# A hybrid decoder layer on one core: when the transfers that sum weight blocks are issued

## The chip, the core and the metric

The kernel runs on one core of a Trainium2 chip. The metric is the device time of one execution in microseconds (us). The core has a matrix engine (PE), a vector engine (DVE), a scalar engine (ACT), a general engine (POOL) and a synchronisation engine (SP) that here only issues DMAs. Each engine takes its instructions in the order of its own queue. Sixteen DMA engines move the bytes; SP and POOL issue to different DMA queues.

## What is computed

One trunk layer over 512 positions of width 1024, in f32:

```python
h = rms_norm(x, norm_mix)
hq, hf, hi, hg, mq, mk, mv = split(h @ w_in)        # 7 x 512 columns
o_hgrn = hgrn2_mixer(hq, hf, hi, hg, lb, hgrn_norm) # gated linear recurrence, 4 heads
o_moba = moba_attention(rotary(mq), rotary(mk), mv) # block-sparse causal attention, 4 heads
x = x + concat(o_hgrn, o_moba) @ w_out
h, mem_n = rms_norm(x, norm_xattn), rms_norm(mem, norm_mem)
x = x + cross_attention(h, mem_n, w_xq, w_xk, w_xv, w_xo)   # 256 memory tokens, 4 heads
h = rms_norm(x, norm_mlp)
x = x + square(relu(h @ w_ff1)) @ w_ff2             # 1024 -> 4096 -> 1024
return rms_norm(x, norm_final)
```

## The kernel before

**Weights come in units.** A unit is 512 KB of a weight matrix, 128 partitions by 1024 f32. It is loaded into a tile `wr` (three buffers), then split for PE into an upper part `wh`, made by ACT with a copy to fp32r, and a lower part `wl = wr - wh`, made by DVE. A product is three matmuls: upper by upper, upper by lower, lower by upper. Units 0 to 27 are the columns of `w_in`, by stage: hf (0 to 3), hi (4 to 7), hq (8 to 11), mv (12 to 15), mkq (16 to 23), hg (24 to 27). Units 28 to 79 follow the list `line`: the eight units of `w_out` (wo), the eight of `w_xq` (xq) and the eight of `w_xo` (xo), with 28 units of the memory's keys and values (`memX`, `memY`) put between those of wo and xq by `AFTER_WO` and `AFTER_XQ`: wo is units 28 to 32, 36, 39 and 43; xq is 46, 49, 52, 55, 58, 62, 65 and 67; xo is 72 to 79. Then follow the two matrices of the MLP.

**How units are fed.** Before the matmuls of unit `w`, `need(w)` issues loads and splits ahead of it. With three raw buffers a unit is split two units ahead and loaded some five ahead; a load waits on SP until `wl` of the unit three before it has been made. `need` also notes in `marks` the last matmul issued so far.

**Sums of weight blocks.** The memory's keys and values and the second MLP matrix are multiplied by a scheme with seven products in place of eight, whose weight operands are sums of blocks. These sums are made in DRAM by DMAs alone. `mem_sums` and `block_sums` list 88 transfers. A copy goes out on SP (line 237). An add, which accumulates into its destination, goes out on POOL (line 240). The pieces of value blocks, two DMAs of 256 KB to a transfer, go out on POOL as well (line 269). In the order of the list:

- 0 to 3 pieces and 4 to 7 adds that make the first memory sum;
- 8 to 11 copies that begin the third memory sum, 12 to 15 pieces that begin the fourth;
- 16 to 19 copies of the first sum into the second, 20 to 27 adds to the second and third, 28 to 31 adds of the second sum to the fourth;
- 32 to 47 copies and 48 to 63 adds for the MLP's sums, 64 to 87 the rest of them.

**Which sets the order.** `load_unit` issues the load of unit `u` and then `sums_after(u)` transfers of the list, by `more_sums`. Each of them is made to wait for `marks[-2]`; for the transfers behind unit `u` that is the end of the matmuls of unit `u - 7`. A copy that waits on SP holds up what stands behind it there, later loads among it. The list's order also carries data: an add waits for the landing of what it adds to, and the loads of the summed units (`wr<-m`, `wr<-u`) for the sums. The very first part, and the MLP, run in an order written out by hand (`manual_schedule`); between them the framework's scheduler orders each engine's queue. `Pace` is the kernel's own estimate of time, by which side work such as attention heads is put among the matmuls; `copy` and `add` go to the engines directly, past its records.

**Side work that the steps touch.** In hq, `ev_q` scales the query of an HGRN2 head into the tiles `qx` and `q` on DVE, and `hgrn_out` multiplies these on PE (tiles `ket`, `a`, `pd`, `ho`). In xq, `xattn_probs` makes scores on PE (`xs`), their minimum on DVE (`xum`), the exponentials on ACT (`xp`), and turns these on PE (`xt`). Nearly every compute instruction is recorded under line 118, the helper that calls the engine, so groups are told apart by their tiles.

Of the kernel before, what the change touches and what calls it, by code (L numbers as in the profile page):

```python
# [31 lines left out]
W_HG, W_WO, W_MEMK, W_XQ, W_MEMV, W_XO, W_MLP = 24, 28, 36, 44, 52, 60, 68  # L32
# [93 lines left out]
def hybrid_layer(ctx: ExitStack, tc: tile.TileContext, xT, memT, ws, vecs, consts, rots, out):  # L126
# [91 lines left out]
    line, keys = [], iter(KEYS + VALUES)  # L218
# [96 lines left out]
    def load_unit():  # L315
        u = state["load"]
        raws[u] = raw_tile(f"wr{u}", u >= FF2 and (u - FF2) % 2 == 1)
        if len(sources[u].shape) == 3:
            SY.dma_start(raws[u].rearrange("p (n c) -> p n c", n=4), sources[u])
        else:  # L320
            SY.dma_start(raws[u], sources[u])
        state["load"] += 1
        for _ in range(sums_after(u)):
            more_sums()

    def sums_after(u):

        if u < W_WO:
            return 2 * (u >= 8) + (u >= 22)
        if u < MLP:  # L330
            return line[u - W_WO][0] in ("wo", "xo")
        return u % 2 == 0 and (4 <= u - FF2 < 14 or u - FF2 >= 26)

    W_MV = 12
# [432 lines left out]
    u = 4  # L767
# [614 lines left out]
    u = MLP  # L1382
# [437 lines left out]
```

## Time and profile before

| | |
|---|---|
| median of 3 runs | 727.66 us (727.19 to 728.85) |
| the profiled execution, its own time | 727.53 us |
| its span, first to last instruction | 725.8 us |
| mean granted clock of PE | 0.992 |
| largest wait of PE | 4.7 us |
| waits of ACT for loads of `wr` | 22.3 us in 16 |

The span is what the trace covers; the time of an execution is some 1.7 us longer. In the views, a row of the timeline gives start and duration in us, then engine, line, operation, what it writes and reads, and in brackets how long the engine was idle before it and what ended that. A row of the waits gives the sum, the count and the longest. A row of the chain of waits gives start, duration, engine and what it worked on. A row of DMA issues gives their count, size, and the median time from issue to landing. `SPq` is SP's own queue. A load's row tells when it was issued, not when it landed.

### The profile page before, as it was taken

How to read it: one execution, taken by the hardware profiler on the slowest of the kernel's cores; microseconds unless marked ns; L12 is line 12 of the kernel's file. 1: busy time of each engine (PE TensorE's matmuls, PEld its weight loads, DVE VectorE, ACT ScalarE, POOL GpSimd, SP SyncE). 2: the span in 40 equal slices, each digit the busy share in tenths (PEclk: the TensorE clock that was granted, in tenths of full speed). 3: DMA queues.
4: the chain of work that ended last, by engine and by line, in shares of the span. 5: the costliest groups of instructions: out<-in, count | busy, mean ns of one | idle time of the engine just before them, and what ended most of it. 6: DMA issues, size and time to landing. Idle time of an engine off the chain costs nothing.

```text
span 725.8 us, 10723 instructions
## 1 busy us (share of the span) xinstructions
PE 712.3 (98%) x4024; PEld 613.6 (85%) x4024; DVE 579.2 (80%) x878; ACT 452.5 (62%) x659; POOL 81.1 (11%) x98
## 2 busy tenths in 40 slices
PE   9997999999999999999999999999999999999995
PEld 7885888888888888888888899999999888888885
DVE  5897635899879676786668799989899999987886
ACT  6873467455777576666656866666567755546672
POOL 1421123000000000001201011111120100110000
PEclk9999999999999999999999999999999999999998
DMA  8798689994557864557997388777989965998523
GB/s 273 239 254 297 197 159 203 348 338 119 145 184 206 243 229 154 174 168 182 262 279 178 99 224 216 210 216 201 220 191 284 290 233 183 278 266 258 179 84 116
DMA packets 62803, 155.71 MB, mean 215 GB/s; under 512 B 5248, under 2 KB 19456, under 8 KB 62240
## 3 DMA queue, kind: packets, MB, share of 16 engines
q1 hardware_dynamic: 47552, 116.70, 46.2%
q0 software_dynamic: 14592, 37.75, 28.8%
q8 instruction: 31, 0.51, 0.3%
q10 hardware_dynamic: 608, 0.59, 0.3%
q14 instruction: 20, 0.16, 0.1%
HBM read 152.92 MB, written 48.23 MB: 277 GB/s over the span
## 4 chain that ended last, share of the span: by engine, by line
PE 90%; DMA 4%; ACT 3%; DVE 2%; issue 1%; DVEq 0%; SPq 0%; ACTq 0%
PE Y L118 16%; PE X L118 12%; PE xo L118 8%; PE XB L118 6%; PE XA L118 6%; PE mkq L118 6%; PE wo L118 6%; PE xq L118 4%; DMA wr<-in_ws_dram 4%; PE mv L118 3%; PE hg L118 3%; PE Z L118 3%; PE hf L118 3%; PE memX L118 3%; PE memY L118 2%; PE hq L118 1%
## 5 line engine op out<-in xcount | busy, mean ns | idle before, releaser
L118 DVE TENSOR_TENSOR wl<-wr,wh 128x1024 fp32r<-128x1024 f32 (+2 forms) x139 | 165.7, 1197 | 39.8 <-ACT wh L118 33.2
L118 ACT ACTIVATE wh<-wr 128x1024 fp32r<-128x1024 f32 (+2 forms) x139 | 142.8, 1037 | 85.3 <-DMA wr<-in_ws_dram 22.3
L240 POOL DMA_DIRECT2D u<-in_ws_dram x32 | 27.4, 874 | 319.1 <-DMA wr<-m 88.3
L118 PE MATMUL X<-op,wh 128*128 128x512 f32 (+1 forms) x264 | 62.9, 385 | 0.0
L118 PEld LDWEIGHTS X<-op,wh 128*128 128x128 f32 x264 | 47.2, 189 | 8.5
L118 PE MATMUL Y<-op,wh 128*128 128x512 f32 x192 | 47.2, 391 | 0.0
L118 PEld LDWEIGHTS Y<-op,wh 128*128 128x128 f32 x192 | 35.0, 189 | 6.5
L118 PEld LDWEIGHTS X<-op,wl 128*128 128x128 f32 x256 | 33.5, 191 | 1.6
L118 PE MATMUL X<-op,wl 128*128 128x256 f32 x256 | 34.1, 283 | 0.0
L118 PE MATMUL Y<-OS,wh 128*128 128x256 f32 x256 | 33.4, 283 | 0.0
L118 PEld LDWEIGHTS Y<-OS,wh 128*128 128x128 f32 x256 | 32.5, 192 | 0.7
L118 DVE TENSOR_TENSOR op<-g,op 128x1024 fp32r<-128x1024 f32 x24 | 29.3, 1220 | 2.8 <-ACT op L118 2.8
L118 ACT ACTIVATE op<-g 128x1024 fp32r<-128x1024 f32 x28 | 29.3, 1045 | 0.6 <-PE XB L118 0.6
L118 ACT ACT_TABLE_LOAD x20 | 25.7, 1283 | 2.1 <-PEq L1808 1.2
L118 PEld LDWEIGHTS Y<-op,wl 128*128 128x128 f32 x192 | 25.3, 191 | 1.3
L118 PE MATMUL Y<-op,wl 128*128 128x256 f32 x192 | 25.7, 282 | 0.0
L118 PE MATMUL mkq<-xlo,wh 128*128 128x512 f32 x64 | 25.7, 401 | 0.0
L118 PE MATMUL xq<-x1hi,wl 128*128 128x512 f32 x64 | 25.6, 400 | 0.0
L118 PE MATMUL mkq<-xhi,wl 128*128 128x512 f32 x64 | 25.4, 396 | 0.0
L118 PE MATMUL xq<-x1hi,wh 128*128 128x512 f32 x64 | 25.3, 396 | 0.0
L118 PE MATMUL mkq<-xhi,wh 128*128 128x512 f32 x64 | 25.3, 395 | 0.0
L118 PE MATMUL xo<-oxhi,wh 128*128 128x512 f32 x64 | 25.1, 393 | 0.0
(384 smaller groups left out, 1908.6 us busy)
## 6 DMA issues: line engine op xcount, KB each, us to landing
wr<-in_ws_dram SPq DMA_DIRECT2D x87, 512.0 KB, 5.5
u<-in_ws_dram POOLq DMA_DIRECT2D x32, 512.0 KB, 7.7
wr<-u SPq DMA_DIRECT2D x32, 512.0 KB, 4.4
u<-in_ws_dram SPq DMA_DIRECT2D x16, 512.0 KB, 12.1
wr<-m SPq DMA_DIRECT2D x16, 512.0 KB, 3.7
m<-in_ws_dram POOLq DMA_DIRECT2D x12, 512.0 KB, 10.6
m<-in_ws_dram POOLq DMA_DIRECT2D x16, 256.0 KB, 7.4
wA<-in_ws_dram SPq DMA_DIRECT2D x8, 512.0 KB, 5.6
```

The source lines that it names most:

```text
L118: return f(*args, **kw)
L240: return nc.gpsimd.dma_start(dst, src, accum_op=ALU.add, max_dma_last_dim=4 * D)
```

## The change

`sums_after(u)` gives other numbers of transfers. Units 12 to 15 have none behind them, where each had two; the eight loads of xq have one each, where they had none. The list and its order, the adds' and copies' queues and the rule of the marks stay. All transfers from the ninth on (number 8) are so attached to later loads, until the counts agree again at the first unit of xo with number 54.

```diff
     def sums_after(u):
 
         if u < W_WO:
-            return 2 * (u >= 8) + (u >= 22)
+            return 2 * (8 <= u < 12 or u >= 16) + (u >= 22)
         if u < MLP:
-            return line[u - W_WO][0] in ("wo", "xo")
+            return line[u - W_WO][0] in ("wo", "xo", "xq")
         return u % 2 == 0 and (4 <= u - FF2 < 14 or u - FF2 >= 26)
```

`W_WO` is 28, `MLP` is 80. The numbers of the transfers behind the loads:

| behind unit | before | after |
|---|---|---|
| 8 to 11 | 0 to 7 | 0 to 7 |
| 12, 13 | 8 to 11 | none |
| 14, 15 | 12 to 15 | none |
| 16, 17 | 16 to 19 | 8 to 11 |
| 18, 19 | 20 to 23 | 12 to 15 |
| 20, 21 | 24 to 27 | 16 to 19 |
| 22 to 25 (three each) | 28 to 39 | 20 to 31 |
| 26, 27 (three each) | 40 to 45 | 32 to 37 |
| the eight of wo | 46 to 53 | 38 to 45 |
| the eight of xq | none | 46 to 53 |
| the eight of xo | 54 to 61 | 54 to 61 |

## The prediction

> **What bounds the kernel now.** First the page: how much of the span TensorE (PE) leaves empty, and which DMA queues carry the weights.
>
> ```profile
> span 725.8 us, 10723 instructions
> PE 712.3 (98%) x4024; PEld 613.6 (85%) x4024; DVE 579.2 (80%) x878; ACT 452.5 (62%) x659; POOL 81.1 (11%) x98
> q1 hardware_dynamic: 47552, 116.70, 46.2%
> q0 software_dynamic: 14592, 37.75, 28.8%
> ```
>
> PE is empty for 13.5 us, so an edit that only moves DMAs can win in two ways: by removing a wait of PE, or by keeping its clock up. The waits of PE and of its weight loads (PEld) name the places.
>
> ```profile
> PE a L118 <- DVE qx L118: 4.7, 1, 4.7
> PEld xt L118 <- ACT xp L118: 0.9, 2, 0.5
> ```
>
> The first is by far the largest. It lies in the stage of unit 8 to 11 (hq), where the decay products `a` of the first HGRN2 head need `qx` from VectorE (DVE). The timelines of PE, DVE and ScalarE (ACT) around it, then the chain that ended last:
>
> ```profile
> 65.06 0.43 PE L118 MATMUL a<-qx,kt 128*32 128x32 f32 x8
> 70.19 0.37 PE L118 MATMUL a<-qx,Fz 128*32 128x96 f32 x3 [4.71 <-DVE qx L118]
> 63.95 0.42 DVE L118 TENSOR_TENSOR qx<-hq,eb 128x256 f32<-128x256 f32 x1
> 68.57 1.23 DVE L118 TENSOR_TENSOR wl<-wr,wh 128x1024 fp32r<-128x1024 f32 x1 [4.20 <-ACT wh L118]
> 69.92 0.22 DVE L118 TENSOR_TENSOR qx<-qx,ee 128x64 f32<-128x64 f32 x1
> 71.25 0.22 DVE L118 TENSOR_TENSOR qx<-qx,ee 128x64 f32<-128x64 f32 x1
> 74.20 0.42 DVE L118 TENSOR_TENSOR q<-qx,pp 128x256 f32<-128x256 f32 x1
> 61.00 0.64 ACT L118 ACTIVATE lnf<-lnf 128x512 f32<-128x512 f32 x1 [0.57 <-DVE lnf L118]
> 67.48 1.06 ACT L118 ACTIVATE wh<-wr 128x1024 fp32r<-128x1024 f32 x1 [5.85 <-DMA wr<-in_ws_dram]
> 52.22 15.16 DMA wr<-in_ws_dram
> 71.53 0.95 PE a L118 x12
> 78.58 1.04 PE a L118 x28
> ```
>
> Read it backwards. PE waits 4.71 us for `qx`. DVE had begun `qx` at 63.95, but next in its queue stands the lower part `wl` of a weight unit, and DVE waits there 4.20 us for the upper part `wh`. ACT could have made that at 61.64, when `lnf` ends; it waits 5.85 us for a load issued at 52.22 that took 15.16 us. Counting loads of `wr` on SP, it is unit 12. PE itself needs that unit only when hq is done: the load hurts because it heads two queues.
>
> The clock pays as well (columns: stretch, its length, busy time of PE, PEld, DVE, ACT, POOL, granted clock, DMA share, GB/s).
>
> ```profile
> 69.00:70.00 1.00, 0.00 (x0) 0.00 (x0) 1.00 (x3) 1.00 (x2) 0.00 (x0) 0.61 0.03 12
> 75.00:76.00 1.00, 1.00 (x6) 0.90 (x6) 0.27 (x1) 0.83 (x2) 0.00 (x0) 0.50 1.02 330
> 76.00:77.00 1.00, 1.00 (x6) 0.83 (x5) 0.78 (x3) 0.08 (x1) 0.00 (x0) 0.98 0.82 276
> ```
>
> PE went idle at 65.49. The grant fell some 3.7 us later (a mean of 0.61 in 69 to 70 puts the fall to 0.5 at about 69.2) and returned at 76.0, 5.8 us after work resumed. The Trainium skill, "TensorE: Matmul & The Clock Gate", section "What's actually happening", says that an idle window of about 3.4 us halves the clock and a busy one of the same length restores it. The fall agrees; the return took 5.8 us here, so the measurement decides, and by the page's figure the gain below would be about 1.2 us smaller, some 723.6 us in all (an estimate).
>
> What made the load slow are the DMAs issued just around it, of SP (line 237) and POOL (line 269):
>
> ```profile
> 40.11 1.33 SPq L237 DMA_DIRECT2D m<-in_ws_dram  x2
> 49.43 2.07 SPq L237 DMA_DIRECT2D m<-in_ws_dram  x2
> 51.26 3.00 POOL L269 DMA_DIRECT2D m<-in_ws_dram  x4 [12.98 <-PE hi L118]
> 56.02 2.94 POOL L269 DMA_DIRECT2D m<-in_ws_dram  x4 [1.75 <-PE hq L118]
> wr<-in_ws_dram SPq DMA_DIRECT2D x7, 512.0 KB, 3.3
> ```
>
> These are exactly transfers 8 to 15 of the sum list, which `sums_after` now gives to units 12 to 15: four copies of 512 KB and eight pieces of 256 KB. The last row, from the DMA answer for 284 to 316 us where no sums run, is the same kind of load undisturbed: 3.3 us.
>
> **The change part by part.** No instruction is added or removed: 88 transfers stay, each on its queue. Transfers 8 to 53 come later in the order of loads, and from the first xo load on both orders agree.
>
> *Units 12 to 15, emptied.* DVE's chain ahead of unit 12's load is untouched, so that still leaves at 52.2. Undisturbed it lands at 55.5; sums 4 to 7 may still linger, but it could take 9.4 us before ACT, free at 61.64, would notice. `wh` ends at 62.7, `wl` starts when DVE reaches it at 64.37, and DVE runs 4.20 us earlier. PE then resumes 4.20 us earlier, at 65.99. The second half of `a` needs the `qx` that ended at 71.47, now 67.27; its 0.95 us at half clock become 0.48, so `a` ends at 67.8 in place of 72.48: 4.7 us. With PE idle under 2 us the clock should stay: the 3.5 us from 72.48 to 76.0 become 1.76. **Gain 4.7 + 1.75 = 6.4 us.** Against it stands DVE, nearly full from 68.6 on, which follows by 4.2 us and perhaps no more. But `a` of the second head starts on PE at 78.58, and its DVE work was done by 74.62 (the `q` of the DVE rows): 4 us of slack take up the other 2.2. I count the full 6.4; the lower end is 4.2.
>
> *Units 16 to 21 (mv and mkq weights are then on PE).* Units 16 and 17 get four DRAM copies in place of four, 18 and 19 small pieces in place of four adds, 20 and 21 copies in place of adds. Twelve adds move to units 22 to 25. From the queue rows 512 KB on q0 take 0.288 x 725.8 / 37.75 x 0.524 = 2.9 us of the sixteen engines, on q1 1.5 us: this stretch gets lighter, then denser.
>
> ```profile
> 85.00:118.00 33.00, 33.00 (x277) 28.11 (x276) 16.29 (x29) 24.73 (x32) 9.26 (x8) 1.00 0.82 157
> 118.00:160.00 42.00, 42.00 (x202) 35.04 (x201) 34.02 (x84) 21.67 (x41) 4.60 (x4) 1.00 1.05 322
> 203.00:262.00 59.00, 59.00 (x264) 48.77 (x262) 46.10 (x58) 41.53 (x59) 2.44 (x3) 1.00 0.71 210
> 262.00:335.00 73.00, 72.91 (x372) 60.81 (x371) 52.38 (x85) 50.77 (x92) 1.62 (x2) 1.00 0.54 170
> wr<-in_ws_dram SPq DMA_DIRECT2D x3, 512.0 KB, 8.8
> ```
>
> The load row is of 85 to 117, where two adds stand beside each load. From 118 to 160 the DMA engines are full already, with copies ahead of the loads on SP; adds go on the other queue instead, so a load there should be nearer that row. PE is never empty in either stretch (33.00 of 33, 42.00 of 42). Zero, covered by loads issued long before PE needs them; 2 us worse if the cover goes.
>
> *wo (unit 28 to 43).* Two copies and six adds become eight copies, 1.5 us each in place of 2.9. PE has no empty time there (59.00 of 59), so the relief is worth nothing. The copies wait on SP for the marks of PE's progress that the adds waited for on POOL, and the next load stands behind them; but a mark lies seven units back and a load is issued some five units ahead, so the mark has passed when SP gets there. Zero; up to 2 us if SP is held.
>
> *xq (unit 46 to 67): the cost.* Two copies and six adds enter a stage with none. Adds go by a mark, the end of the matmuls seven units earlier. The third is due after unit 51:
>
> ```profile
> 278.56 0.39 PE L118 MATMUL memY<-wh,mo 128*128 128x512 f32 x1
> 276.75 5.80 DMA wr<-in_ws_dram
> 282.63 1.07 ACT wh L118
> 283.73 1.23 DVE wl L118
> 284.95 0.34 DVE xum L118
> 286.68 0.44 PE xt L118 x2
> 267.46 1.06 ACT L118 ACTIVATE wh<-wr 128x1024 fp32r<-128x1024 f32 x1
> wr<-m SPq DMA_DIRECT2D x1, 512.0 KB, 4.2
> ```
>
> This is the hq pattern again: the load of unit 55 holds `wh`, `wl` stands in DVE's queue before `xum`, and PE's transposes `xt` wait. PE's slack is nil: that is the 0.9 us in the waits. The add leaves at about 279.2, when 3.3 of the load's 5.8 us remain. Ends: nothing, if it moves its bytes after 282.5; the add's whole 2.9 us, if the load gets no turn meanwhile. I take just under half, **1.3 us**. Below nothing is excluded, as nothing on this chain gets earlier but ACT's `wh` of 267.46, which had no wait. That one is unit 50 (last row: issued at 262.22, landed 266.42, 1.04 us early); a copy and an add beside it can eat this and more, 0 to 3.4 us; I take 0, since units 39 to 45 load faster now and their chain arrives earlier.
>
> **Sum:** 727.53 (the profiled execution; span 725.8 and 1.7 around it; the median shown is 727.66) - 6.4 + 1.3 = **722.4 us**.
>
> **The rivals.**
> 1. *The adds take equal turns with the loads.* Unit 55 then pays 2.9 us, unit 50 0.5 beyond its slack: 727.5 - 6.4 + 3.4 = 724.5. For it: loads beside adds took 8.8 us against 3.3. Against: only the last part of the load is met. The Trainium skill, "DMA: Bandwidth & Descriptors", section "Queues, rings and completion order", says that each engine goes round the queues that have work, packet by packet; by that rule this rival wins. That loads among adds are slow, not starved, agrees.
> 2. *The wait stays.* The moved copies of units 16 and 17 need only PE's end of units 9 and 10, and the order on SP is the scheduler's here, not the written one: it may put them ahead of loads that still wait for a buffer. Or another load heads DVE's queue instead, unit 13's say. Time 727.5, or up to 1.5 less. Against: unit 12 has some 6 us of room.
> 3. *Slower: the clock falls in xq.* If PE stands over 3.7 us at `xt`, the hq dip is repeated: 5.8 us at half clock, 2.9 lost. At a delay of 5 us the loss is 7.9, the gain is spent: 727.5 - 6.4 + 7.9 = 729.0; this decides from 3.7 us on. All copies and adds at full price on units 47, 50 and 55 make 7.8 us, thus at most 731.8. For it: nil slack. Against: it needs every transfer to fall wrong.
>
> **How the numbers follow.** Forecast 0.60 (its own range 720.2 to 724.6: a free or dearer xq, DVE's 4.2), rival 1 0.20, rival 2 0.08, rival 3 0.09, and 0.03 for a larger gain. The range 720.2 to 726.4 takes the first two. A measurement of this kernel tells about 0.2%, 1.5 us, from no change: faster (below 726.2) 0.82, within 0.09, slower 0.09.
>
> **What would show it.** Right: unit 12's load under 8 us, PE's wait for `qx` under 1 us, the clock 1.00 from 62 to 88 us, and a new wait of PE at `xt` of 1 to 2 us. Wrong: a load over 10 us before `qx`; a clock under 0.9 near 285; PE empty time in mkq (over 105 us), where the twelve adds land.

## The result and the profile after

The changed kernel takes 722.64 us, the median of six runs (720.61 to 724.72), against 728.08 us (727.19 to 729.83) for the kernel before on the same chip. The ratio is 0.9927, with a 95% interval of 0.9903 to 0.995: faster by some 0.7%. Single executions that took 879 us or more, at most two of a kernel, are left out of all medians and ratios below. The execution that was profiled took 724.72 us, the slowest of the six; why it was so matters below.

First the page of the changed kernel, then its waits of PE. The counts of the engines' work are those of before.

```profile
span 722.9 us, 10727 instructions
PE 711.8 (98%) x4024; PEld 613.3 (85%) x4024; DVE 578.6 (80%) x878; ACT 451.3 (62%) x659; POOL 81.1 (11%) x98
```

```profile
PE XB L118 <- DVE g L118: 1.7, 1, 1.7
PE xt L118 <- ACT xp L118: 0.5, 1, 0.5
PE a L118 <- DVE qx L118: 0.2, 1, 0.2
```

The 4.7 us at `qx` have become 0.2, and a wait of 1.7 us stands in the MLP that was not there. The timelines of DVE and ACT in hq show why the first went:

```profile
63.03 0.42 DVE L118 TENSOR_TENSOR qx<-hq,eb 128x256 f32<-128x256 f32 x1
63.37 1.22 DVE L118 TENSOR_TENSOR wl<-wr,wh 128x1024 fp32r<-128x1024 f32 x1
```

```profile
60.08 0.63 ACT L118 ACTIVATE lnf<-lnf 128x512 f32<-128x512 f32 x1 [0.56 <-DVE lnf L118]
60.62 1.99 ACT L118 ACTIVATE wh<-wr 128x1024 fp32r<-128x1024 f32 x2
```

ACT makes the upper parts of units 12 and 13 back to back right behind `lnf`, with no bracket: it waits for nothing. DVE's `wl` has no bracket either. The load of unit 12, from the DMA answer for the stretch in which it alone is issued, and the clock (columns as in the same view of before, whose row for these 26 us is the second fence):

```profile
wr<-in_ws_dram SPq DMA_DIRECT2D x1, 512.0 KB, 3.4
```

```profile
62.00:88.00 26.00, 21.28 (x250) 17.39 (x249) 17.16 (x52) 8.45 (x12) 2.15 (x2) 0.87 0.65 225
```

```profile
62.00:88.00 26.00, 25.69 (x311) 21.54 (x313) 19.61 (x51) 11.28 (x18) 3.00 (x4) 1.00 0.61 203
```

The load takes 3.4 us in place of 15.16. PE is busy 25.69 of 26 us in place of 21.28, at a granted clock of 1.00 in place of a mean of 0.87. The 4.4 us less of empty time, and the half clock, at which PE had worked from 70.19 to 76.05 and lost half of these 5.9 us, add up to 7.3 us: that is the gain.

Where it went from there is read from PE's timelines: the start of a stage is the start of the first matmul into its tile. The table gives these starts before, and how far after and the changed kernel's two repeats (`a1_again`, `a2_again`, below) stand from them, in us. Minus is earlier.

| first matmul of | before | after | a1_again | a2_again |
|---|---|---|---|---|
| `a` (in hq) | 65.06 | -0.14 | -0.02 | +0.97 |
| `mv` | 85.39 | -7.29 | -7.33 | -6.35 |
| `wo` | 203.43 | -7.28 | -7.32 | -6.34 |
| `xq` | 261.09 | -7.32 | -7.36 | -6.38 |
| `xt` (in xq) | 286.68 | -6.47 | -6.81 | -6.63 |
| `xo` | 337.87 | -6.35 | -6.80 | -6.61 |
| `XB` (MLP) | 413.78 | -6.34 | -6.81 | -6.64 |
| `X` (second MLP matrix) | 560.78 | -2.79 | -6.80 | -6.63 |
| end of span | 725.75 | -2.81 | -6.80 | -6.63 |

So the change wins some 7.2 us between `a` and `mv`, keeps them through mkq, hg and wo, gives back up to 1 us in xq (nothing in `a2_again`), and in the one execution that was profiled first 3.5 us more are lost in the MLP, where the order of the transfers is the same as before. Neither repeat shows that last loss.

### The profile page after: what moved, and what is told of

Its sections match the earlier page's. It is cut to its first block, busy times and chain, and to the rows that moved or that the text cites. A ratio compares the mean times of both kernels' runs of the same rounds, so it can differ in the third digit from the quotient of the medians.

```text
span 722.9 us, 10727 instructions
## 1 busy us (share of the span) xinstructions
PE 711.8 (98%) x4024; PEld 613.3 (85%) x4024; DVE 578.6 (80%) x878; ACT 451.3 (62%) x659; POOL 81.1 (11%) x98
## 4 chain that ended last, share of the span: by engine, by line
PE 86%; DVE 5%; DMA 4%; ACT 3%; issue 1%; DVEq 0%; POOL 0%; ACTq 0%; POOLq 0%
PE Y L118 15%; PE X L118 12%; PE xo L118 8%; PE mkq L118 6%; PE XB L118 6%; PE XA L118 5%; PE wo L118 5%; PE xq L118 4%; PE mv L118 3%; PE hf L118 3%; PE hg L118 3%; PE Z L118 3%; PE memX L118 2%; DVE wl L118 2%; PE memY L118 2%; DMA wr<-in_ws_dram 2%
## 5 line engine op out<-in xcount | busy, mean ns | idle before, releaser
L118 PE MATMUL xq<-x1lo,wh 128*128 128x512 f32 x64 | 25.2, 393 | 0.0
```

The source lines that it names most:

```text
L118: return f(*args, **kw)
```

## The experiments

Each kernel was timed beside the kernel before on the same chip. Ratios have 95% intervals.

| kernel | median us | ratio |
|---|---|---|
| the change, again (a1_again) | 721.07 | 0.9892 [0.9864, 0.9919] |
| DVE's order alone (e1_order) | 727.76 | 0.9974 [0.9953, 0.9995] |
| xq for wo (e2_xq_for_wo) | 731.06 | 1.0024 [1.0006, 1.0041] |
| wo twice (e3_wo_twice) | 724.34 | 0.9933 [0.9908, 0.9958] |
| DVE's and ACT's order (e1b_both) | 723.01 | 0.9924 [0.9897, 0.9951] |
| rest at units 14 and 15 only (e4_rest_14_15) | 721.87 | 0.9918 [0.9893, 0.9944] |
| transfers late in xq (e5_xq_late) | 723.58 | 0.9938 [0.9916, 0.9961] |
| the change, one MLP sum later (e6_f1_last) | 722.26 | 0.9917 [0.9893, 0.994] |
| the change, a third time (a2_again) | 721.48 | 0.9916 [0.9887, 0.9945] |
| both orders, one MLP sum later (e8_orders_last) | 720.75 | 0.9905 [0.988, 0.9929] |
| both orders and the change (e9_after_orders) | 721.22 | 0.991 [0.9883, 0.9937] |

### What held PE up in hq: a transfer, or what queued behind it

The prediction says that unit 12's late load hurts only because `wl` stands ahead of `qx` on DVE and `wh` ahead of other work on ACT. If so, the wait goes without moving any transfer when these instructions stand further back. `e1_order` is the kernel before with the lower parts of units 12 and 13 put on DVE behind the last `q` issued until then; in its trace the `q` of the first two heads go ahead of unit 12's. `BEHIND` orders two instructions of one engine without a semaphore.

```diff
         def lower(hi=his[u], lo=los[u]):
-            (eng or V).tensor_sub(lo[:, a:b], raw[:, a:b], hi[:, a:b].bitcast(F32))
+            low = (eng or V).tensor_sub(lo[:, a:b], raw[:, a:b], hi[:, a:b].bitcast(F32))
+            if u in (W_MV, W_MV + 1):
+                tc.add_manual_dep(low.ins, last_q[0].ins.name, BEHIND)
...
-            V.tensor_mul(q4[:, t0 * P:(t0 + 2) * P].rearrange("p (t c s) -> p t c s", c=4, s=CHUNK),
+            last_q[0] = V.tensor_mul(q4[:, t0 * P:(t0 + 2) * P].rearrange("p (t c s) -> p t c s", c=4, s=CHUNK),
```

> The kernel before, no transfer moved; on DVE the lower parts wl of units 12 and 13 go behind the qx and q of the first two heads. Theory (the late load costs only because wl stands in front of qx in DVE's queue): unit 12's load is as late as before (landing near 67), PE's wait for qx falls from 4.7 to under 1 us, the clock stays at 1.00 from 62 to 88 us, time 720.5 to 722.5 (6 to 7 us under before). Rival (the transfers slow hq in more ways than this queue): PE waits elsewhere in hq, gain under 3 us, 725 to 728.

It missed: `mv` starts 1.31 us earlier, not 6 or 7, and the time is 0.9974 of before. The wait at `qx` is gone, but PE's timeline and then ACT's show another in its place.

```profile
70.88 1.65 PE L118 MATMUL pd<-Vh,kets 128*128 128x128 f32 x6 [3.72 <-ACT kets L118]
```

```profile
68.08 1.06 ACT L118 ACTIVATE wh<-wr 128x1024 fp32r<-128x1024 f32 x1 [7.05 <-DMA wr<-in_ws_dram]
69.39 1.06 ACT L118 ACTIVATE wh<-wr 128x1024 fp32r<-128x1024 f32 x1 [0.26 <-DMA wr<-in_ws_dram]
70.35 0.47 ACT L118 ACTIVATE kets<-ket 128x384 f32<-128x384 f32 x1
```

`kets`, the first operand that PE needs from ACT after `a`, stands behind both `wh`. ACT waits 7.05 us for the same load, now 16.4 us long, and PE 3.72 us for ACT; the clock falls to 0.50 again at 70.2. The load headed two queues, and clearing one only showed the other. `e1b_both` therefore also puts both `wh` behind the first head's `kets` on ACT:

```diff
+        if u in (W_MV, W_MV + 1):
+            early_wh.append(rounded)
...
-        A.activation(ket[:, :3 * P], pt[:, :3 * P], AF.Copy)
+        turned = A.activation(ket[:, :3 * P], pt[:, :3 * P], AF.Copy)
+        if h == 0:
+            for made_high in early_wh:
+                tc.add_manual_dep(made_high.ins, turned.ins.name, BEHIND)
```

> The kernel before, no transfer moved. On DVE the lower parts wl of units 12 and 13 go behind the qx and q of the first two heads, and on ACT their upper parts wh go behind kets, the copy that PE's pd waits for. With the DVE order alone PE's 4.7 us at qx became 3.7 us at pd, for kets stood behind wh on ACT. Theory (the late load costs by standing ahead in two queues): unit 12's load is still late (landing 66 to 68), PE waits under 1 us in hq, the clock stays 1.00, mv's first matmul comes 6 to 7.5 us earlier than in the trace of before (at 78 to 79.4 us), time 720.5 to 723. Rival (a third queue or PE itself waits for the late units): mv's first matmul after 82 us, time over 725.

Unit 12's load and the stretch of hq in this kernel:

```profile
wr<-in_ws_dram SPq DMA_DIRECT2D x1, 512.0 KB, 15.0
```

```profile
60.00:90.00 30.00, 30.00 (x365) 25.54 (x364) 23.42 (x66) 14.06 (x22) 2.44 (x3) 1.00 0.91 277
```

The load still takes 15.0 us, and PE has not one empty moment. `mv` starts 7.29 us earlier, and the time is 0.9924. That the change's first trace has the same 7.29 is chance, as `a` starts 0.68 us later in this execution: counted from `a` the orders gain 7.97 us, the change 7.15 to 7.32. The orders gain more since no `wl` stands between the four groups of the first head's `a` any more, which take 1.04 us here and 1.90 in the changed kernel. So the queues are the cause: the transfers only decide how late the instruction at their head can start. Nor do the two remedies add: `e9_after_orders`, with both, gains the same 7.97 us counted from `a`, with `mv` 7.30 us and the end 7.29 us earlier.

> The changed kernel with both orders of e1b as well. If the two remedies act on the same wait, they do not add: mv's first matmul at 77 to 78.2 us, the 0.5 to 1 us of xq stay, time within 1 us of the changed kernel of this call. If units 12 and 13 also cost something behind the queues, 1 to 3 us less.

The 0.5 to 1 us that it expected to lose in xq didn't come: from `xq` to `xo` it loses 0.04.

### Which of the eight transfers made the load late

`e4_rest_14_15` is the kernel before with only the pieces behind units 14 and 15 (POOL's eight DMAs of 256 KB) taken away; the copies behind 12 and 13 stay. Four loads of xq take the four transfers.

```diff
-            return 2 * (u >= 8) + (u >= 22)
+            return 2 * (8 <= u < 14 or u >= 16) + (u >= 22)
...
-            return line[u - W_WO][0] in ("wo", "xo")
+            return line[u - W_WO][0] in ("wo", "xo") or line[u - W_WO] in [("xq", n) for n in range(4, 8)]
```

> Only units 14 and 15 rest (the eight pieces on POOL move on); units 12 and 13 keep their four copies on SP, and only the last four loads of xq take a transfer. If the pieces slow unit 12's load, it lands by 62 and the whole gain in hq stays: mv's first matmul at 78 to 79, time 720.5 to 723. If the copies ahead of it in SP's ring are enough, it lands after 63 and part or all of the wait at qx stays: mv's first matmul at 80 to 85, time 723 to 728.

```profile
wr<-in_ws_dram SPq DMA_DIRECT2D x1, 512.0 KB, 11.4
```

The load of unit 12 takes 11.4 us, PE waits 1.3 us in two places, the clock stays at 1.00, and `mv` starts 5.21 us earlier (5.74 counted from `a`, which was 0.53 later in this execution). With the pieces gone the load is 3.8 us shorter than before; the other 8.0 of its 11.8 us too many stay with the copies. Yet it is not unit 12's load that costs PE the 1.3 us. Two rows of ACT, for units 11 and 12, then the same two units on DVE:

```profile
59.20 1.06 ACT L118 ACTIVATE wh<-wr 128x1024 fp32r<-128x1024 f32 x1 [3.50 <-DMA wr<-in_ws_dram]
63.12 1.06 ACT L118 ACTIVATE wh<-wr 128x1024 fp32r<-128x1024 f32 x1 [0.33 <-DMA wr<-in_ws_dram]
60.30 1.23 DVE L118 TENSOR_TENSOR wl<-wr,wh 128x1024 fp32r<-128x1024 f32 x1 [1.63 <-ACT wh L118]
65.44 1.22 DVE L118 TENSOR_TENSOR wl<-wr,wh 128x1024 fp32r<-128x1024 f32 x1
```

DVE waits for nothing at unit 12. It waits 1.63 us at unit 11, whose load takes 10.8 us here, and all its work for `a` comes later by that. The copies 10 and 11 leave on SP right behind that load. In the six traces of kernels that keep them there it takes 7.9 to 10.9 us, in the seven without them 4.5 to 6.1. So the pieces are worth the larger part of the gain, and what the copies cost beyond them came through the load of unit 11 in this execution.

### What the transfers cost in xq

`e2_xq_for_wo` takes the transfers from wo and gives them to xq, with hq as before, so the cost of xq stands alone.

```diff
-            return line[u - W_WO][0] in ("wo", "xo")
+            return line[u - W_WO][0] in ("xq", "xo")
```

> The kernel before with the eight transfers of wo's loads moved to xq's; units 12 to 15 keep theirs. Theory: hq as before (PE waits 4.7 us), xq pays the 1 us that the changed kernel paid there, 728.5 to 729.5. Within it: if copy 46 ahead of unit 47's load is what costs, that load takes 6 to 7 us in place of 4.3 and DVE waits 2 to 3 us more for it; if the add after unit 51 is what costs, unit 55's load takes over 7 us in place of 5.8. Rival (nothing is paid in xq, the changed kernel's 1 us had another cause): 727 to 728.

The kernel is slower by 0.24%, with an interval that just excludes no change. From `xq` to `xo` it loses 2.0 us (+0.30 to +2.31): PE waits 1.6 us at `xt`, for `xp`. The place is the forecast one, the path is not. The add leaves 1 us after the load of unit 55, on which I had put the cost, but this load takes the 5.8 us of before here, and 4.9 in the changed kernel; the two loads behind it, of units 56 and 57, grow (8.3 and 7.3 us against 5.5 and 4.8). The late ones that count are units 47 and 50, the first with a copy issued ahead of it (6.9 and 5.8 us here). SP's timeline in the changed kernel, then the DMA answers for unit 47's load alone in the changed kernel and before:

```profile
245.81 0.50 SPq L237 DMA_DIRECT2D u<-in_ws_dram  x1
246.56 4.26 SPq L118 DMA_DIRECT2D wr<-in_ws_dram  x3
```

```profile
wr<-in_ws_dram SPq DMA_DIRECT2D x1, 512.0 KB, 7.2
```

```profile
wr<-in_ws_dram SPq DMA_DIRECT2D x1, 512.0 KB, 4.3
```

What that does to DVE, in the timelines of the changed kernel and of before, is the `wl` of that unit:

```profile
254.94 1.23 DVE L118 TENSOR_TENSOR wl<-wr,wh 128x1024 fp32r<-128x1024 f32 x1 [2.99 <-ACT wh L118]
```

```profile
260.96 1.23 DVE L118 TENSOR_TENSOR wl<-wr,wh 128x1024 fp32r<-128x1024 f32 x1 [0.94 <-ACT wh L118]
```

DVE waits 2.05 us more there; unit 50's load follows (5.6 us against 4.2), and what is left of the delay reaches PE at `xt`. The chain of waits that ended last in the changed kernel goes through the loads of units 47, 50 and 55 (some of its rows):

```profile
246.56 7.18 DMA wr<-in_ws_dram
256.19 5.59 DMA wr<-m
271.17 4.92 DMA wr<-in_ws_dram
277.26 1.23 DVE wl L118
280.21 0.44 PE xt L118 x2
```

The other traces with the same transfers agree. Unit 47's load takes 6.2 us in `a1_again`, and 0.55 us are lost from `xq` to `xt`; it takes 5.1 to 5.4 in `a2_again`, `e6_f1_last` and `e9_after_orders`, where nothing is lost on this way. To test the path, `e5_xq_late` is the changed kernel without transfers behind the first two loads of xq, and with two behind each of the last two:

```diff
-            return line[u - W_WO][0] in ("wo", "xo", "xq")
+            name, n = line[u - W_WO][:2]
+            return name in ("wo", "xo") or 2 * (name == "xq" and n > 5) + (name == "xq" and 1 < n < 6)
```

> The changed kernel, but the eight transfers of xq go one each to its third to sixth load and two each to its seventh and eighth; the first two have none. Theory (copies 46 and 47 ahead of the loads of units 47 and 50 cost the 0.5 to 1 us in xq): those loads take 4 to 4.5 us again, the shift of PE's stages against before stays at -7.3 us through xq where the changed kernel's went to -6.3 and -6.8, time 0.5 to 1 us under it. Rival (the add after unit 51, now a copy or a later add, costs it): unit 55's load above 5.8 us, xt still 0.5 to 1 us late.

The first half came as the reading of units 47 and 50 has it: their loads take 3.3 and 3.5 us, and `xt` still starts 7.36 us earlier (`xq` 7.53). But the time is 0.9938, no better. The doubled transfers cost 2.7 us between `xt` and `xo` (-7.36 to -4.62), where the waits of PE show two new ones:

```profile
PE xs L118 <- DVE xql L118: 0.8, 1, 0.8
PE xt L118 <- DVE PT L118: 0.6, 1, 0.6
```

The eight transfers have no free place in xq: put late they cost more than put early.

### Is there room in wo instead?

The prediction costed wo at nothing. `e3_wo_twice` is the changed kernel with the transfers of xq put behind wo's loads, two each.

```diff
-            return line[u - W_WO][0] in ("wo", "xo", "xq")
+            return {"wo": 2, "xo": 1}.get(line[u - W_WO][0], 0)
```

> Units 12 to 15 rest as in the changed kernel, but wo's loads get two transfers each and xq's none. Theory: the gain in hq stays (6.4 to 7.2 us), xq pays nothing, wo has room (PE never empty there): 1 us under the changed kernel where the MLP agrees, 720 to 721.5. Rival (wo has no room: units 39 to 43 have under 2 us between wl and PE): a wait of PE in wo or at xq's start, 722 to 725.

No. `mv` starts 7.08 us earlier, `memX` 7.10, but `xq` only 3.03: 4.1 us are lost before xq begins. PE's waits, then the stretches around them (columns as before):

```profile
PE memY L118 <- ACT wh L118: 1.1, 1, 1.1
PE memY L118 <- DVE wl L118: 0.8, 1, 0.8
```

```profile
244.00:246.00 2.00, 0.93 (x4) 0.37 (x2) 0.32 (x1) 1.18 (x2) 0.00 (x0) 1.00 1.02 377
246.00:248.00 2.00, 1.24 (x6) 0.87 (x6) 2.00 (x3) 1.40 (x2) 0.00 (x0) 1.00 0.15 47
248.00:250.00 2.00, 2.00 (x7) 1.54 (x6) 1.90 (x3) 2.00 (x4) 0.00 (x0) 0.55 0.85 253
```

1.8 us of idle time in two pieces, and then the clock is at 0.55: the waits themselves are under half of the loss. The trace has the clock at half from 248.22 to 251.63, 3.41 us with PE busy throughout, which is 1.7 us more. One transfer to a load is hidden in wo, two are not.

### The loss in the MLP

> The changed kernel once more, for more executions and a second trace. In its first trace 3.5 us were lost in the first MLP matrix, where the load wd took 10.1 us (7.3 before) and PE then waited 1.7 us at a lower clock. Theory (a chance of the execution): the second trace has wd at 7 to 8 us, no wait of PE there and a span of about 719.5 us, and the times lie in two groups some 3.5 us apart, 720.5 to 721.5 and 724 to 725. Rival (the change causes it): wd late again, PE waits 1.5 to 2 us again, span 722 to 723, all times above 722.

The repeat has no such loss: it ends 6.80 us earlier than before, as `xo` starts. The two groups of times didn't come: its five executions took 720.16 to 722.07 us. In the first profile of the change, DVE waits 4.0 us for the tile `wd`, the last block of the first MLP matrix. DVE's timeline there and PE's stretches:

```profile
544.97 1.23 DVE L118 TENSOR_TENSOR wd<-wd,wA 128x1024 f32<-128x1024 f32 x1 [3.95 <-DMA wd<-in_ws_dram]
546.11 1.22 DVE L118 TENSOR_TENSOR wl<-wc,wh 128x1024 fp32r<-128x1024 f32 x1
547.25 0.68 DVE L118 TENSOR_TENSOR g<-g,XB 128x512 f32<-128x512 f32 x1
```

```profile
546.00:548.00 2.00, 0.26 (x4) 0.05 (x2) 2.00 (x4) 1.72 (x2) 0.81 (x1) 1.00 0.03 12
548.00:550.00 2.00, 2.00 (x9) 2.00 (x10) 2.00 (x2) 0.28 (x1) 0.00 (x0) 0.54 0.96 160
550.00:552.00 2.00, 2.00 (x7) 1.53 (x7) 1.93 (x3) 0.07 (x1) 0.00 (x0) 0.60 1.01 281
```

It is the hq pattern a third time: a late load heads DVE's queue, `g` stands behind it, PE is idle for 1.7 us, and the clock halves, from 548.17 to 551.59. The load of `wd` takes 10.1 us in this execution, 7.3 before, 7.5 and 7.2 in the repeats, and 8.8 in `e1_order`, where DVE waits 2.8 us and PE loses 1.5 with no transfer moved. So it comes and goes with the execution, in either order of the transfers: of the eleven traces with an add on POOL just ahead of this load, only these two lose more than 0.1 us there against before. `e6_f1_last` is the changed kernel with this add moved into the second MLP matrix:

```diff
-        if s == 2:
+        if s == 2 and j < 7:
             more_sums()
...
-        return u % 2 == 0 and (4 <= u - FF2 < 14 or u - FF2 >= 26)
+        return u % 2 == 0 and (4 <= u - FF2 < 16 or u - FF2 >= 26)
```

> The changed kernel without the transfer that is issued on POOL just ahead of the last load wd of the first MLP matrix; it goes behind unit 14 of the second matrix instead. Theory (that add makes wd late in some executions, and PE then waits and loses its clock): DVE's wait for wd under 1 us, no wait of PE at XB, the times of the changed kernel near 724.7 do not appear: median 720 to 721.5 and a spread under 2 us. Rival (wd is late by chance whatever stands before it): times up to 724 to 725 again.

The load of `wd` takes 4.9 us and nothing waits for it; the times lie between 721.28 and 722.83, narrower than the 720.61 to 724.72 of the change, but no narrower than `a1_again`, which has the add in place. The median, 722.26, is no better and missed the forecast 720 to 721.5. On one chip with another repeat of the change (`a2_again`) stands the version that leaves hq's transfers alone, orders both queues as `e1b_both` does and has this edit too (`e8_orders_last`):

> The changed kernel a third time, as the measure for the two others of this call on one chip: a ratio of 0.989 to 0.993 to before, 720 to 725. Theory that wd's late load is a chance of the execution: DVE's wait for wd under 2 us in this trace with odds of about three to one.

> No transfer of the early stages moved: both orders of e1b (DVE and ACT serve the first heads before units 12 and 13), and the add ahead of wd put behind unit 14 of the second MLP matrix. Theory: hq as in e1b (mv's first matmul 7.3 us earlier), no loss in xq, no late wd: 0.5 to 1.5 us under the changed kernel of this call, 719.5 to 722. Rival (executions differ by more than that): the same as the changed kernel within its interval.

`wd` loads in 4.3 us in `e8_orders_last`, against 6.9 to 10.1 in the eleven traces with the add: that the add lengthens this load is shown, that it causes the rare loss is likely and not shown. The kernel ends 7.44 us earlier than before, against 6.63. Its median of 720.75 us is the lowest of all and 0.7 us under the change on the same chip, but their ratios, 0.9905 and 0.9916, lie well inside each other's intervals. It is as good as the change; that it is better is not shown.

## Why the prediction was right, and where it was not

Forecast were 722.4 us, a range of 720.2 to 726.4 and a faster kernel; measured were 722.64. The sum came out close; its terms less so.

**Units 12 to 15, a gain of 6.4.** The mechanism was right: the load under 8 us (3.4), PE's wait under 1 us (0.2), the clock at 1.00, and the 2.2 us that DVE might not have followed did come. Counted from `a`, the gain in the three traces of the change is 7.15, 7.31 and 7.32, so the term was 0.7 to 0.9 too small. The sum was worked out on one trace, and took DVE to reach `qx` in the changed kernel as late against PE as there. But in the trace of before ACT waits once more, earlier, for unit 8's load:

```profile
39.64 1.06 ACT L118 ACTIVATE wh<-wr 128x1024 fp32r<-128x1024 f32 x1 [0.85 <-DMA wr<-in_ws_dram]
```

DVE runs that much later from there on: its first `qx` starts 1.11 us before PE's first `a`, in the three traces of the change 1.89, 2.05 and 2.06. The first of the moved copies leaves only at 40.11. Three of the six traces of kernels that keep copies 8 to 11 where they were have this wait, none of the seven others; whether more than chance is behind that stays open.

The clock's part, 1.75 us, came (from the end of the first head's `a` to `mv` PE needs 1.70 us less). Its premise, "With PE idle under 2 us the clock should stay", was not tested in hq, where PE had 0.3 us of idle time; in the MLP it failed at 1.74 us.

**mkq, hg and wo, nothing.** Right: the shift stays within 0.1 us from `mv` to `xq` in all three traces. The side remark that the relief in wo is worth nothing was right too, but it was not to be read as room for more, as `e3_wo_twice` shows.

**xq, a cost of 1.3.** Too high, and by another path. From `xq` to `xo` the three traces of the change lose 0.97, 0.56 and -0.23 us (a gain), `e6_f1_last` 0.79 and `e9_after_orders` 0.04, with the same transfers there; `e2_xq_for_wo` alone loses 2.0. Four kernels without transfers in xq lie between -0.49 and 0.43. The wait of 1 to 2 us at `xt` that I asked for was 0.5 in the first trace. The step that failed is the one behind "The add leaves at about 279.2, when 3.3 of the load's 5.8 us remain": in `e2_xq_for_wo` it left at 279.8, and unit 55's load got no longer. The step that I had taken at 0, "a copy and an add beside it can eat this and more", with a range of 0 to 3.4, was the one that paid, through unit 47's load and unit 50's. I had looked at the load that already hurt, and not at the first one to follow the new copy on its own queue. Both errors go the same way: at `XB`, ahead of the place of the MLP's loss, the three traces are 6.34, 6.81 and 6.64 us earlier than before, where the sum has 6.4 - 1.3 = 5.1. That the sum came within 0.3 us of the median is partly luck.

**The rivals.** The first, equal turns on unit 55, fell with that path: 724.5 was its time, and this load took no more than before, though an add on the other queue was under way for most of it. The Trainium skill, "DMA: Bandwidth & Descriptors", section "Queues, rings and completion order", has the queues served in turn, packet by packet; by that rule the prediction had unit 55's load grow beside the add, and here it didn't (5.8 us with it and without), while the loads of units 56 and 57 were longer and not starved (8.3 and 7.3 us). Unit 47's load and the copy ahead of it stand on one queue, so the page's rule doesn't bear on it. The second, the wait stays, fell by unit 12's 3.4 us; its half sentence that something else may head the queue is what `e1_order` then showed. The third put its price on a clock that falls only when "PE stands over 3.7 us at `xt`". At `xt` it never stood so long. But the threshold was wrong, as the MLP and `e3_wo_twice` show (a fall with 1.7 us of idle time), and so was the price of 5.8 us at half clock: there it was 3.41 us. A fall of the clock was more likely than I thought; the last section has what decides it.

**What was not in the sum.** The MLP's loss of 3.5 us, which made the first profiled execution the slowest of its six. Nothing of the change reaches there: both orders agree from the first load of xo on. By that execution alone, 724.72, the sum would seem 2.3 us too low; the repeats and the median show that it was not.

## What to carry to other kernels

A load that PE doesn't need for a long time can still stop PE, when the instruction that reads it stands at the head of an in-order queue ahead of what PE does need. Follow the wait back to the load, then ask of each queue that it heads what stands behind: here two queues had to be cleared, or the load made early. Background transfers cost nothing only where each load next to them has time in hand, and that has to be read load by load, beginning with the first load behind the new transfer on its own queue.

## What the hardware showed unexpectedly

**The clock is decided in fixed stretches of 3.41 us, by how much PE works in each.** The changes of the granted clock that the traces hold lie on a grid. Before the change it fell at 69.22 and came back at 76.05, two times 3.41 us later, and it fell again, after PE's last work, at 721.17, which is 191 times 3.413 us after 69.22. In all five traces with a fall inside the program, that fall and the one at the end lie a whole number of 3.413 us apart (50, 138, 191, 191 and 192), and the clock stays low for 3.41 or 6.83 us. Stretches of this grid, the first three before the change, the fourth in the first trace of the change, the fifth in `e3_wo_twice`, the last in `e2_xq_for_wo` at `xt`:

```profile
65.81:69.22 3.41, 0.00 (x0) 0.00 (x0) 0.65 (x1) 1.56 (x2) 0.00 (x0) 1.00 0.51 205
69.22:72.63 3.41, 2.43 (x49) 1.72 (x50) 3.41 (x13) 0.94 (x2) 0.00 (x0) 0.50 0.48 168
72.63:76.05 3.42, 3.42 (x12) 2.94 (x13) 2.64 (x6) 1.31 (x2) 0.00 (x0) 0.50 0.96 302
544.76:548.17 3.41, 1.67 (x14) 1.46 (x13) 3.20 (x4) 3.03 (x4) 0.81 (x1) 1.00 0.25 64
244.81:248.22 3.41, 1.76 (x7) 1.23 (x7) 2.54 (x3) 2.57 (x4) 0.00 (x0) 1.00 0.52 163
286.88:290.29 3.41, 1.86 (x12) 1.44 (x11) 1.37 (x6) 2.52 (x9) 0.00 (x0) 1.00 0.95 323
```

The clock fell at the end of the stretches in which PE was busy for 0.00, 1.67 and 1.76 us (also 0.36 in `e1_order` and 1.31 in `e2_xq_for_wo`, both in hq). It stayed after 1.86, and after 2.04 (`e4_rest_14_15`) and 2.24 us (`e1_order`, MLP). It came back after a stretch in which PE was busy throughout, five times of five, and not after 0.32, 2.43 or 2.74. So in these traces the line lies at about half a stretch, and where a wait falls on the grid, which differs between executions, decides too. The 3.7 us to the fall and the 5.8 us to the return that the prediction read before the change are such places on the grid and no fixed delays.

The Trainium skill ("TensorE: Matmul & The Clock Gate", section "What's actually happening") gives a free-running window of about 3.4 us, with which the grid agrees, and a fall after an idle window; here windows in which PE had worked for half of the time were enough, and the measurement decides. For pricing, an estimate from these rows: a single wait under 1.5 us, with PE busy around it, keeps the clock, one over 3.3 us loses it, and between them it is a matter of place; a fall costs at least half of 3.41 us, which doubled the loss in the MLP (1.7 us of waiting, 3.5 us lost).

**One load's time differs by 3 us between executions of one program.** That of `wd`, with the same add ahead of it, took 10.1, 7.5 and 7.2 us in three executions of the changed kernel. In the first DVE waited 4.0 us for it and the total lost 3.5; in the second DVE waited 1.5 us and nothing was lost. A single profile can contain such a loss or not, so a change of 1% should be read stage by stage in more than one trace.
